# Last square of the second norm summed on TensorE and its spread read from PSUM; query and key transposes moved to the two banks of the scores

## The chip, the core and the metric

The kernel runs on one core of a Trainium2 chip. It is one program. The metric is its time on the device in microseconds (us). Before the change the median of three runs is 3415.19 us (3414.32 to 3415.7).

## The reference

Two transformer-like blocks run one after the other on one sequence of 512 tokens, width 1024, in float32. The first block has a conv branch, a gated linear recurrence (hgrn) and a stick-breaking attention, merged by gates, and after it a norm and a squared-ReLU feed-forward. The second block has two layers, each with a SwiGLU feed-forward, a mixer of softmax attention with a forget gate beside an RG-LRU recurrence, and a second SwiGLU. Cut to what the change touches:

```python
# first block, between its mixer and its feed-forward
x = x + g1 * (merged @ w_out[l])
h2 = rms_norm(x, norm2_g[l]) * (1.0 + sc2) + sh2      # mean of squares over the 1024 channels
x = x + g2 * (square(relu(h2 @ mlp_w1[l])) @ mlp_w2[l])

# second block, the mixer of each of two layers
q = rms_norm_2(q.reshape(B, S, 8, 128), q_norm[l])    # per head
k = rms_norm_2(k.reshape(B, S, 8, 128), k_norm[l])
y_attn = forgetting_attention(q, k, v, log_f) @ w_o_attn[l]
xr = causal_depthwise_conv(xr, conv_w[l], conv_b[l])  # 4 taps
yr = rg_lru(xr, ...) * gelu(gr)                       # two gates, then a scan over the positions
```

## The kernel before

Activations are held transposed: a tile `x` has 128 channels on the partitions and the 512 tokens in the free dimension, and the width of 1024 is eight such tiles. Weights stream from HBM in chunks of 128x512. Each chunk lands in a `raw` tile, ScalarE casts it to `hi` (line 197) and VectorE takes the rest `lo = raw - hi` (line 198); the ring of `raw`, `hi` and `lo` holds four chunks each. A product is three TensorE matmuls into an accumulator `a` (lines 229 to 231). There are four accumulators `a`, one PSUM bank each; the other four banks are, in the second block, one `xm`, one `xh` and two `xs` (`self.banks(..., xm=1, xh=1, xs=2)` in `run`); in the first block they are two `xh` and two `xs`.

**Order.** A tile belongs to a tag with a number of buffers. Tiles of one tag take the buffers in turn, in the order in which the program asks for them, and a tile waits until the tile that had its buffer before is read for the last time. When the kernel is built, a scheduler fixes the order of instructions on every engine by its own timing; work under `self.hp()` is taken first when ready, the rest in program order. On the chip each engine follows its fixed order and waits at an instruction whose inputs are not there, with all that stands behind it.

**The second norm.** `add_square` squares each new `x` tile on ScalarE (line 300) and adds it to the running sum `p` on VectorE (line 308). `stats` sums `p` over the partitions on TensorE (`rows_of`, line 272), takes the power -1/2 on GpSimd (line 281), spreads the row of factors over the partitions by four transposes (`spread`, line 289) and copies them from PSUM to the tile `rb` (line 291). Then eight `t` (line 588) and `h` (lines 590 and 591) are made from it, and the feed-forward's products read `h`.

**The mixer of the second block.** In `mix`, the recurrence `rnn` asks for its tiles first: per channel tile j = 0 to 7 a convolution of four taps on VectorE into `xc` (lines 893 and 895), two gate matmuls into two `xs` tiles (lines 897 and 898), a tanh of each (lines 900 and 901), an exponential, a second tanh and a square on ScalarE (lines 902, 903, 300), and two combining operations on VectorE (lines 905 and 906). After each four tiles come the square roots (line 911), and on VectorE a multiplication (913) and a scan over the positions (914). `xc` has three buffers and is also the tile of the square, so that tile j+2 of the convolution reuses what tile j held.

Then, for each half `hf` of the heads, the tokens of query, key and value are computed (`tokens`, four accumulators, eight chunks). VectorE takes them out of PSUM (line 1027), for query and key into `qk` tiles, of which there are five. `heads_T` norms them (lines 300, 381, 383, 384, 388) and transposes them on TensorE, four 128x128 blocks per tile, into a PSUM tile (line 393) that ScalarE copies to `qkT` (line 395). `attn` then runs 16 steps per half: scores into `xs` (line 830), softmax (833 to 841), transposes of the weights into `xs` (851), a copy (853) and the values into `xh` (855). While it runs, TensorE fills in the products that stand next in the program: those of the gelu gate, then query, key and value of the second half.

Of the kernel before, what the change touches and what calls it, by code (L numbers as in the profile page):

```python
# [16 lines left out]
D, S, F1, F2 = 1024, 512, 4096, 2816  # L17
# [7 lines left out]
def _cols(name, l, kt, c0):  # L25
    return [(name, l, k, 2, c0, 256) for k in range(0, kt, 2)]
# [6 lines left out]
def _plan_first():  # L33
    p = []
    for k in range(8):
        p += [("w_in", 0, k, 1, 1280, 512), ("w_in", 0, k, 1, 1792, 256)]
    p += _cols("w_in", 0, 8, 1024)
    p += _rows("w_in", 0, 8, 2048)
    for c in (512, 0, 768, 256):
        p += _cols("w_in", 0, 8, c)  # L40
    for c in (3072, 3584, 4096):
        p += _rows("w_in", 0, 8, c)
    for c in (2560, 2816):
        p += _cols("w_in", 0, 8, c)
    for b, w in BRANCHES:
        for m in range(0, 8, 2):
            p += _cols("w_in", 0, 8, 4608 + b * 1024 + m * 128)
            p += _cols(w, 0, 4, m * 128)
    for m in range(0, 8, 2):
        p += _cols("w_out", 0, 8, m * 128)  # L50
    for hf in range(2):
        for f in range(0, 16, 4):
            p += _both(*[_cols("mlp_w1", 0, 8, (hf * 16 + f + e) * 128) for e in (0, 2)])
        for m in range(0, 8, 2):
            p += [("mlp_w2", 0, hf * 16 + k, 2, m * 128, 256) for k in range(0, 16, 2)]
    return p
# [62 lines left out]
class Build:  # L119
# [148 lines left out]
    def rows_of(self, p, scale, xt="xm"):  # L268
# [4 lines left out]
                                  start=True, stop=True)  # L273
        return ps[:, 0:4]

    def rsqrt(self, src, w, g="m"):

        nc = self.nc
        m, r = self.small(w, g), self.small(w, g)
        nc.vector.tensor_scalar(m, src, EPS, None, op0=OP.add)  # L280
        nc.gpsimd.tensor_tensor(r, m, self.mhalf[:, :w], op=OP.pow)
        return r

    def spread(self, rt, xt="xm", tr="rb"):

        nc = self.nc
        ps = self.aux(xt)
        for i in range(4):
            nc.tensor.transpose(ps[:, i * 128:i * 128 + 128], rt[:, i:i + 1].to_broadcast([128, 128]), self.ident)
        rb = self.t(tr)  # L290
        nc.scalar.copy(rb, ps)
        return rb
# [83 lines left out]
    def heads_T_(self, src, nh, dh, gain):  # L376
        nc = self.nc
        ms, m, r = [self.small(4 * nh) for _ in range(3)]
        for tt in range(4):
            sq = self.square(src[tt], "t")  # L380
            nc.vector.tensor_reduce(ms[:, tt * nh:tt * nh + nh], sq.rearrange("p (h d) -> p h d", d=dh),
                                    op=OP.add, axis=AX.X)
        nc.vector.tensor_scalar(m, ms, 1.0 / dh, EPS, op0=OP.mult, op1=OP.add)
        nc.gpsimd.tensor_tensor(r, m, self.mhalf[:, :4 * nh], op=OP.pow)
        for tt in range(4):
            y = src[tt].rearrange("p (h d) -> p h d", d=dh)
            rr = r[:, tt * nh:tt * nh + nh][:, :, None].to_broadcast([128, nh, dh])
            nc.vector.tensor_tensor(y, y, rr, op=OP.mult)
        out = []
        for j in range(4):  # L390
            ps = self.aux("xm" if "xm" in self.pxt else "xs")
            for tt in range(4):
                nc.tensor.transpose(ps[:, tt * 128:tt * 128 + 128], src[tt][:, j * 128:j * 128 + 128], self.ident)  # L393
            o = self.t("qkT")
            nc.scalar.activation(o, ps, AF.Copy, scale=gain)
            out.append(o)
        return out
# [163 lines left out]
    def first_block(self):  # L561
        nc = self.nc
        src = lambda i: self.ap["xT"][i * 128:i * 128 + 128, :]
        with ExitStack() as ctx:
            fp = ctx.enter_context(self.tc.tile_pool(name="fp", bufs=1))
            self.banks(ctx, xh=2, xs=2)
            self.stream("w_first", _plan_first())
            self.mod = self.lined(fp, (128, 48), name="mod")
            self.cs = self.lined(fp, (128, 1024), name="cs")
            with ExitStack() as c1:  # L570
                mg = self.first_mix(c1, fp, src)
                with self.hp():
                    mh = [self.split(y, "Y") for y in mg]
                    self.load_x(src)
                x = self.x
                for m in range(0, 8, 2):
                    for i, a in enumerate(self.pair("w_out", 0, 8, m * 128, mh)):
                        with self.hp():
                            nc.vector.scalar_tensor_tensor(x[m + i], a, self.mod[:, 16 + m + i:17 + m + i], x[m + i],
                                                           op0=OP.mult, op1=OP.add)  # L580
                            self.add_square(x[m + i], m + i == 0)
            self.pool(ctx, "mlp", act=32, t=4, mr=2)
            with self.hp():
                _, rb = self.stats()
                h2 = []
                for i in range(8):
                    y, sh = self.t("t"), self.mod[:, 24 + i:25 + i]
                    nc.vector.scalar_tensor_tensor(y, x[i], self.mod[:, 32 + i:33 + i], rb, op0=OP.mult, op1=OP.mult)
                    hi, lo = self.t("h", F32R), self.t("h", F32R)
                    nc.scalar.activation(hi, y, AF.Identity, bias=sh)  # L590
                    nc.vector.scalar_tensor_tensor(lo, y, sh, hi.bitcast(F32), op0=OP.add, op1=OP.subtract)
                    h2.append((hi, lo))
            self.later("mod", [lambda j=j: self.mod_rest(j) for j in range(24, 32)], 0.2)
            self.later("mod", [self.decay_rates], 0.2)
            for hf in range(2):
                act = []
                for f in range(0, 16, 4):
                    for a in self.pairs(*[_cols("mlp_w1", 0, 8, (hf * 16 + f + e) * 128) for e in (0, 2)], h2):
                        y = self.t("t")
                        with self.hp():  # L600
                            nc.scalar.activation(y, a, AF.Relu)
                            nc.vector.tensor_tensor(y, y, y, op=OP.mult)
                            act.append(self.split(y, "act"))
                for m in range(0, 8, 2):
                    accs = [self.acc(), self.acc()]
                    for k in range(0, 16, 2):
                        self.cols(accs, ("mlp_w2", 0, hf * 16 + k, 2, m * 128, 256), hf * 16, hf * 16 + 15, act)
                    for i, a in enumerate(accs):
                        with self.hp():
                            nc.vector.scalar_tensor_tensor(x[m + i], a, self.mod[:, 40 + m + i:41 + m + i], x[m + i],  # L610
                                                           op0=OP.mult, op1=OP.add)
                            if hf:
                                self.ready(m + i, ("ffn1_norm_2", 0))
# [558 lines left out]
```

## Time and profile before

| | before |
|---|---|
| median of three runs | 3415.19 us |
| profiled execution | 3415.62 us |
| its span | 3413.8 us |
| busy: TensorE, VectorE, ScalarE, GpSimd | 3393.3, 1880.3, 1308.8, 164.6 us |
| granted TensorE clock, mean | 0.997 |

The profile is of one execution; its own time is 1.8 us above its span, and 0.43 us above the median. Its page gives the busy time of each engine, the chain of work that ended last and the costliest groups of instructions. A busy share of a matmul engine counts overlapping, pipelined matmuls, so how long a matmul holds the engine is read from the distance between the starts of two rows in the timeline, not from the duration in one row. A value in square brackets at the end of a timeline row is the time that the engine idled before it, with what ended the wait.

### The profile page before, as it was taken

Reading aid. Unit: us, or ns where it says so; the run is one execution under the profiler, and the core shown is the slowest. Engines: PE = TensorE matmul, PEld = TensorE weight load, DVE = VectorE, ACT = ScalarE, POOL = GpSimd, SP = SyncE. Lnnn points to the kernel's source line nnn. Section 1 sums busy time; section 2 is a strip of 40 time slices with the busy share of each in tenths; the row PEclk is TensorE's granted clock in tenths of the full one; section 3 lists DMA queues with packets and bytes.
Section 4 is the critical chain, followed back from the end, with each engine's and each line's share of the span. In section 5 each row is a group of like instructions: output and inputs, shape, how many; then the busy total and the mean of one; then the engine's idle time right before and its main releaser. Section 6 shows DMA issues by size and latency. Waiting matters only on the chain.

```text
span 3413.8 us, 42019 instructions
## 1 busy us (share of the span) xinstructions
PE 3393.3 (99%) x15370; PEld 2769.7 (81%) x15370; DVE 1880.3 (55%) x3168; ACT 1308.8 (38%) x2284; POOL 164.6 (5%) x273
## 2 busy tenths in 40 slices
PE   9999999999999999999999999999999999999999
PEld 6887777888888888788888888888887788888887
DVE  7698654534444444876455444444447865454442
ACT  3335443423333333654333333333336544343331
POOL 0011100000000001121000000000010110000000
PEclk9999999999999999999999999999999999999999
DMA  6223533433333333232333333333333222433332
GB/s 217 72 75 105 155 112 111 130 96 97 98 95 94 97 118 106 89 91 90 112 96 96 97 98 96 96 97 99 102 124 94 87 90 81 122 95 99 96 104 91
DMA packets 179599, 351.30 MB, mean 103 GB/s; under 512 B 20672, under 2 KB 21952, under 8 KB 178368
## 3 DMA queue, kind: packets, MB, share of 16 engines
q1 hardware_dynamic: 172944, 328.53, 31.5%
q0 software_dynamic: 6160, 19.37, 1.9%
q8 instruction: 121, 1.98, 0.2%
q10 hardware_dynamic: 288, 0.72, 0.1%
q14 instruction: 86, 0.70, 0.1%
HBM read 342.21 MB, written 6.32 MB: 102 GB/s over the span
## 4 chain that ended last, share of the span: by engine, by line
PE 97%; DVE 2%; ACT 1%; issue 0%; DMA 0%; POOL 0%; SPq 0%; DVEq 0%; ACTq 0%
PE a L231 30%; PE a L229 30%; PE a L230 30%; PE xh L855 1%; PE xs L830 1%; PE xh L430 1%; PE xh L512 1%; PE xs L490 1%; PE xs L851 1%; PE xm L393 0%; DVE xc L895 0%; PE xh L506 0%; PE xh L469 0%; PE xs L897 0%; PE xs L898 0%
## 5 line engine op out<-in xcount | busy, mean ns | idle before, releaser
L198 DVE TENSOR_TENSOR lo<-raw,hi 128x512 fp32r<-128x512 f32 x1144 | 785.8, 688 | 1255.9 <-ACT hi L197 1240.4
L197 ACT CAST hi<-raw 128x512 fp32r<-128x512 f32 x1144 | 707.1, 619 | 1569.4 <-PE a L230 1271.2
L230 PE MATMUL a<-h,hi 128*128 128x512 f32 x2528 | 990.3, 392 | 0.0
L229 PE MATMUL a<-h,hi 128*128 128x512 f32 x2528 | 984.6, 392 | 2.3 <-ACT h L590 2.3
L231 PE MATMUL a<-h,lo 128*128 128x512 f32 x2528 | 983.3, 393 | 0.0
L229 PEld LDWEIGHTS a<-h,hi 128*128 128x128 f32 x2528 | 475.5, 188 | 106.1 <-issue 6.1
L231 PEld LDWEIGHTS a<-h,lo 128*128 128x128 f32 x2528 | 475.2, 188 | 105.4 <-issue 7.2
L230 PEld LDWEIGHTS a<-h,hi 128*128 128x128 f32 x2528 | 475.2, 188 | 101.5 <-issue 3.6
L229 PE MATMUL a<-act,hi 128*128 128x512 f32 x960 | 373.4, 389 | 0.0
L230 PE MATMUL a<-act,hi 128*128 128x512 f32 x960 | 373.4, 389 | 0.0
L231 PE MATMUL a<-act,lo 128*128 128x512 f32 x960 | 372.8, 389 | 0.0
L230 PE MATMUL a<-Y,hi 128*128 128x512 f32 x544 | 214.5, 394 | 0.0
L229 PE MATMUL a<-Y,hi 128*128 128x512 f32 x544 | 213.7, 393 | 0.0
L231 PE MATMUL a<-Y,lo 128*128 128x512 f32 x544 | 212.8, 391 | 0.0
L230 PEld LDWEIGHTS a<-act,hi 128*128 128x128 f32 x960 | 180.2, 188 | 37.4
L229 PEld LDWEIGHTS a<-act,hi 128*128 128x128 f32 x960 | 180.2, 188 | 37.4
L231 PEld LDWEIGHTS a<-act,lo 128*128 128x128 f32 x960 | 180.2, 188 | 37.4
L231 PE MATMUL a<-hi,h 128*128 128x512 f32 x512 | 204.6, 403 | 0.0
L230 PE MATMUL a<-lo,h 128*128 128x512 f32 x512 | 203.7, 398 | 0.0
L229 PE MATMUL a<-hi,h 128*128 128x512 f32 x512 | 199.2, 407 | 1.7 <-DVE qk L1027 1.7
L231 PEld LDWEIGHTS a<-Y,lo 128*128 128x128 f32 x544 | 102.2, 188 | 23.6 <-issue 2.1
L230 PEld LDWEIGHTS a<-Y,hi 128*128 128x128 f32 x544 | 102.1, 188 | 22.9 <-issue 2.0
(290 smaller groups left out, 3056.7 us busy)
## 6 DMA issues: line engine op xcount, KB each, us to landing
raw<-in_w_l SPq DMA_DIRECT2D x852, 256.0 KB, 2.6
raw<-in_w_first SPq DMA_DIRECT2D x284, 256.0 KB, 2.6
mr<-in_mod_b_ SPq DMA_DIRECT2D x32, 512.0 KB, 3.8
mq<-in_mod_a SPq DMA_DIRECT2D x8, 1024.0 KB, 7.5
xs<-x POOLq DMA_DIRECT2D x16, 256.0 KB, 2.3
cb<-cd POOLq DMA_DIRECT2D x16, 256.0 KB, 3.5
x<-xs POOLq DMA_DIRECT2D x16, 256.0 KB, 3.8
bq<-in_brow POOLq DMA_DIRECT2D x12, 256.0 KB, 3.8
```

Source lines behind the costliest of these rows:

```text
L197: nc.scalar.copy(hi, raw)
L198: nc.vector.tensor_tensor(lo, raw, hi.bitcast(F32), op=OP.subtract)
L229: mm(acc, w[0], x[0], start=start, stop=False)
L230: mm(acc, w[0], x[1], start=False, stop=False)
L231: mm(acc, w[1], x[0], start=False, stop=stop)
L430: mm(ps[:, i * 64:i * 64 + 64], k[:, s], q[:, s].rearrange("p (n c h) -> p n c h", c=2, h=h)[:, :, 1], start=True, stop=True)
L490: mm(z[:, o:o + n], q[pr, blk(i)], k[pr, :n], start=True, stop=True)
L512: mm(pt[pr, c], v[j][:, hd * 64:hd * 64 + 64], f[:, o + j * 128:o + j * 128 + 128], start=j == 0, stop=j == i, skip_group_check=True)
L830: nc.tensor.matmul(ps[:, :n], qT[:, ts], kT[:, :n], start=True, stop=True)
L851: nc.tensor.transpose(pt[:, js], st[:, js], self.ident)
L855: nc.tensor.matmul(o[:, i * 128:n], v[j][:, vc:vc + 128], pT[:, j * 128:j * 128 + 128], start=(i == 0 and j == 0), stop=(i == 3 and j == 3 ...
```

## The change

In the second norm the eighth square is no longer added on VectorE. TensorE sums over the partitions both the sum of the first seven squares and the eighth square, eight matmuls of one column into the same accumulator columns, and the spread factors stay in PSUM, where the eight operations of line 588 read them. In `heads_T_` the PSUM tile of the query and key transposes is always of the tag `xs`; before, it was `xm` where that tag exists, which is in the second block, and `xs` in the first.

```diff
+    def rows_of_sum(self, parts, scale, xt):
+
+        ps = self.aux(xt)
+        for n, p in enumerate(parts):
+            for i in range(4):
+                self.nc.tensor.matmul(ps[:, i:i + 1], p[:, i * 128:i * 128 + 128], self.ones[scale][:, 0:1],
+                                      start=n == i == 0, stop=n == len(parts) - 1, skip_group_check=True)
+        return ps[:, 0:4]
...
-    def spread(self, rt, xt="xm", tr="rb"):
+    def spread(self, rt, xt="xm", tr="rb", out=True):
...
+        if not out:
+            return ps
         rb = self.t(tr)
         nc.scalar.copy(rb, ps)
         return rb
...
-            ps = self.aux("xm" if "xm" in self.pxt else "xs")
+            ps = self.aux("xs")
             for tt in range(4):
                 nc.tensor.transpose(ps[:, tt * 128:tt * 128 + 128], src[tt][:, j * 128:j * 128 + 128], self.ident)
...
-                            self.add_square(x[m + i], m + i == 0)
+                            if m + i < 7:
+                                self.add_square(x[m + i], m + i == 0)
...
-                _, rb = self.stats()
+                ps = self.rows_of_sum([self.p, self.square(x[7])], 1.0 / D, "xh")
+                rb = self.spread(self.rsqrt(ps, 4), "xh", out=False)
```

Lines behind the edits have other numbers in the changed kernel: 393 becomes 404, 897 and 898 become 910 and 911, 905 and 906 become 918 and 919, 913 and 914 become 926 and 927, 1027 becomes 1040, 851 and 855 become 864 and 868. The edit to the transposes also moves instructions. The first place is TensorE in the mixer of the first layer, first half of the heads. Here `xs` pairs with `xc,bd` are the gate matmuls of the recurrence's tiles 5, 6 and 7, rows from `qk` are transposes of the query, and `a` rows are products of the value tokens. Before:

```order
L897 MATMUL xs_11107<-xc_11102,bd_10639 128x512
L898 MATMUL xs_11108<-xc_11102,bd_10647 128x512
L229 MATMUL a_11646<-hi_11652,h_9922 128x512
...
L393 MATMUL xm_11423<-cst,qk_11380 128x128
...
L393 MATMUL xm_11430<-cst,qk_11386 128x128
L229 MATMUL a_11647<-hi_11652,h_9922 128x512
...
L897 MATMUL xs_11127<-xc_11122,bd_10639 128x512
L898 MATMUL xs_11128<-xc_11122,bd_10647 128x512
...
L897 MATMUL xs_11147<-xc_11142,bd_10639 128x512
L898 MATMUL xs_11148<-xc_11142,bd_10647 128x512
```

And now:

```order
L910 MATMUL xs_11108<-xc_11103,bd_10640 128x512
L911 MATMUL xs_11109<-xc_11103,bd_10648 128x512
L229 MATMUL a_11647<-hi_11653,h_9923 128x512
...
L910 MATMUL xs_11128<-xc_11123,bd_10640 128x512
L911 MATMUL xs_11129<-xc_11123,bd_10648 128x512
L910 MATMUL xs_11148<-xc_11143,bd_10640 128x512
L911 MATMUL xs_11149<-xc_11143,bd_10648 128x512
L404 MATMUL xs_11410<-cst,qk_11381 128x128
...
L404 MATMUL xs_11417<-cst,qk_11381 128x128
...
L404 MATMUL xs_11431<-cst,qk_11387 128x128
L229 MATMUL a_11648<-hi_11653,h_9923 128x512
```

Before, there are products between the pairs of tiles 5, 6 and 7 (39 `a` rows between 5 and 6, and 51 between 6 and 7, with transposes among them). Now 12 `a` rows stand between tiles 5 and 6, none between 6 and 7, and all 16 transposes of the query follow in one piece before the next `a` row.

The second place is VectorE at the same time. `xc` rows are taps of the convolution (tile 6 in the first fence, tile 7 in the second), `abc` rows with `xc` are the combining operations, `hm` rows the scans, and the rows into `qk` take key tokens 1 to 3 out of PSUM. Before:

```order
L893 TENSOR_SCALAR xc_11122<-xr_10982,cv 128x512
...
L895 SCALAR_TENSOR_TENSOR xc_11122<-xr_10982,cv,xc_11122 128x512
L1027 SCALAR_TENSOR_TENSOR qk_11589<-a_11440,m_10617,bq_11437 128x512
L1027 SCALAR_TENSOR_TENSOR qk_11591<-a_11441,m_10617,bq_11437 128x512
L1027 SCALAR_TENSOR_TENSOR qk_11593<-a_11442,m_10617,bq_11437 128x512
```

And now:

```order
L908 SCALAR_TENSOR_TENSOR xc_11143<-xr_10988,cv,xc_11143 128x512
L918 SCALAR_TENSOR_TENSOR abc_11133<-xc_11139,abc_11133 128x512
L908 SCALAR_TENSOR_TENSOR xc_11143<-xr_10988,cv,xc_11143 128x512
L919 SCALAR_TENSOR_TENSOR abc_11132<-abc_11132,xc_11123 128x512
L908 SCALAR_TENSOR_TENSOR xc_11143<-xr_10988,cv,xc_11143 128x512
...
L927 SCALAR_TENSOR_TENSOR hm_11094<-hm_11094,abc_11092 128x512
...
L926 TENSOR_TENSOR abc_11152<-abc_11152,abc_11153 128x512
L927 SCALAR_TENSOR_TENSOR hm_11134<-hm_11134,abc_11132 128x512
L1040 SCALAR_TENSOR_TENSOR qk_11590<-a_11441,m_10618,bq_11438 128x512
```

Key tokens 1 to 3 left PSUM during the convolution of tile 6 before; now they stand behind the whole recurrence: the convolutions of tiles 6 and 7, four multiplications and three scans.

The third place is TensorE at the end of the attention of the first half, with the query transposes of the second half. Rows 864 transpose the weights of a step, rows 868 are its values, and `a_12798` and `a_12799` are the first two accumulators of the second half's value tokens. Before, where rows 855 are the values, 851 the weights and `a` rows products of the key tokens:

```order
L393 MATMUL xm_12560<-cst,qk_12531 128x128
L229 MATMUL a_12592<-hi_12650,h_10155 128x512
...
L393 MATMUL xm_12567<-cst,qk_12531 128x128
...
L855 MATMUL xh_12018<-pT_12063,v_11794 128x128
...
L393 MATMUL xm_12574<-cst,qk_12531 128x128
...
L393 MATMUL xm_12581<-cst,qk_12537 128x128
L855 MATMUL xh_12018<-pT_12089,v_11800 128x128
```

And now:

```order
L868 MATMUL xh_12112<-pT_12157,v_11795 128x128
...
L864 MATMUL xs_12162<-cst,s_12141 128x128
L404 MATMUL xs_12561<-cst,qk_12532 128x128
...
L864 MATMUL xs_12162<-cst,s_12141 128x128 x3
L404 MATMUL xs_12568<-cst,qk_12532 128x128
...
L868 MATMUL xh_12112<-pT_12167,v_11795 128x128
...
L404 MATMUL xs_12582<-cst,qk_12538 128x128
L229 MATMUL a_12799<-hi_12804,h_9923 128x512
```

Before, the same transposes were spread over the third of the half's four heads, with `a` rows between them; now they stand at the end of the fourth, with no `a` row among them. The second layer has the same order at the same places.

## Rows read from the trace of the kernel before

**Rows 1.** The page, its chain of work that ended last, by engine.

```profile
PE 97%; DVE 2%; ACT 1%; issue 0%; DMA 0%; POOL 0%; SPq 0%; DVEq 0%; ACTq 0%
```

**Rows 2.** Waits of TensorE in total: engine, line, releaser, us, times, longest.

```profile
PE a L229 <- DVE qk L1027: 1.7, 2, 0.9
...
PE xm L393 <- ACT qkT L395: 0.8, 2, 0.4
```

**Rows 3.** Timeline at the second norm: start, us, engine, line, tiles, [idle before].

```profile
586.97 0.68 DVE L308 TENSOR_TENSOR p<-p,sq 128x512 f32<-128x512 f32 x1
...
589.00 1.02 PE L272 MATMUL xh<-oned,p 128*128 128x1 f32 x8 [2.74 <-DVE p L308]
...
592.55 0.59 ACT L291 COPY rb<-xh 128x512 f32<-128x512 f32 x1 [4.77 <-PE xh L289]
593.17 2.74 DVE L588 SCALAR_TENSOR_TENSOR t<-x,mod,rb 128x512 f32<-128x512 f32 x4 [2.95 <-ACT rb L291]
...
597.22 0.63 PE L231 MATMUL a<-h,lo 128*128 128x512 f32 x1
...
597.65 0.63 PE L229 MATMUL a<-h,hi 128*128 128x512 f32 x1
```

**Rows 4.** Stretches behind it: engines' busy us, granted clock, DMA share, GB/s.

```profile
596.00:600.00 4.00, 4.00 (x11) 2.84 (x10) 4.00 (x7) 1.47 (x4) 0.00 (x0) 0.50 0.02 4
600.00:604.00 4.00, 4.00 (x18) 3.23 (x18) 4.00 (x7) 3.06 (x5) 0.00 (x0) 0.96 0.00 0
```

**Rows 5.** Timeline of TensorE, first layer, transposes and gates among the products.

```profile
1410.02 0.60 PE L393 MATMUL xm<-cst,qk 128*128 128x128 f32 x4
1410.46 1.02 PE L897 MATMUL xs<-xc,bd 128*128 128x512 f32 x2
1411.32 1.02 PE L898 MATMUL xs<-xc,bd 128*128 128x512 f32 x2
1411.78 0.80 PE L229 MATMUL a<-hi,h 128*128 128x512 f32 x1
1412.41 0.39 PE L230 MATMUL a<-lo,h 128*128 128x512 f32 x1
1412.64 0.39 PE L231 MATMUL a<-hi,h 128*128 128x512 f32 x1
...
1423.67 1.02 PE L897 MATMUL xs<-xc,bd 128*128 128x512 f32 x2
```

**Rows 6.** Timeline of VectorE in the same stretch.

```profile
1392.94 1.29 DVE L913 TENSOR_TENSOR abc<-abc,abc 128x512 f32<-128x512 f32 x2
...
1397.72 2.34 DVE L914 TENSOR_TENSOR_SCAN hm<-hm,abc 128x512 f32<-128x512 f32 x2
...
1408.88 0.75 DVE L895 SCALAR_TENSOR_TENSOR xc<-xr,cv,xc 128x512 f32<-128x512 f32 x1
1409.54 0.75 DVE L1027 SCALAR_TENSOR_TENSOR qk<-a,m,bq 128x512 f32<-128x512 f32 x1
...
1414.08 0.69 DVE L906 SCALAR_TENSOR_TENSOR abc<-abc,xc 128x512 f32<-128x512 f32 x1 [1.35 <-ACT abc L901]
```

**Rows 7.** Timeline of ScalarE in the same stretch.

```profile
1389.71 1.28 ACT L911 ACT_TABLE_LOAD   x1
1391.00 2.20 ACT L911 ACTIVATE abc<-abc 128x512 f32<-128x512 f32 x4
...
1411.94 0.68 ACT L900 ACTIVATE abc<-xs,hb 128x512 f32<-128x512 f32 x1
...
1415.18 0.67 ACT L395 ACTIVATE qkT<-xm,qg 128x512 f32<-128x512 f32 x1
...
1424.73 0.69 ACT L900 ACTIVATE abc<-xs,hb 128x512 f32<-128x512 f32 x1 [0.24 <-PE xs L897]
```

**Rows 8.** Timeline of one attention step of the first half, softmax of 512 columns.

```profile
1512.15 0.71 ACT L839 ACTIVATE s<-s,m 128x512 f32<-128x512 f32 x1
...
1513.18 0.49 DVE L841 TENSOR_SCALAR s<-s,m 128x512 f32<-128x512 f32 x1
```

## The prediction

> **What bounds the kernel now.** I read the chain of waits first: 97% of it is TensorE [rows 1]. Then the waits of TensorE: in the mixer of the second block it waits only four times in the whole run, twice 0.86 us for VectorE taking a key token out of PSUM and twice 0.38 us for ScalarE emptying the one transpose bank [rows 2]. So a change is worth what it takes from or adds to TensorE's waits; time on another engine counts only where TensorE reaches an instruction whose inputs that engine has not made. Last, the timelines of the three places that the order shows to be changed. Prices are distances between starts: a product 0.23 us, a gate matmul 0.86 (two rows), four transposes 0.44, and the first product behind a gate pair 0.63 instead of 0.23 [rows 5].
>
> **The second norm.** The chain here is serial, and TensorE waits in it. One VectorE addition goes, but TensorE gets eight sums where it had four: the four of `p` can start when the sixth addition ends (586.97 + 0.68, against 589.00: with the hop 1.2 us sooner), and the added four cost about 1 us (the old four are eight matmul rows in 1.02) [rows 3]. I take 0.3 us gained; between 1 us gained (the sums of `p` fully hidden) and nothing. The copy to `rb` goes: line 588 starts 0.62 us after that copy did [rows 3], and can now start about there: 0.6 us gained. An operation of 588 from PSUM is bounded by 1027, which reads PSUM and takes 0.75 us, against 2.74 us for four of 588, 0.69 each: nothing to 0.06 us on the first one. Sum: 0.9 us gained.
>
> **Transposes, first half of the heads (twice, once in each layer).** On `xm` the transposes depended only on the tokens. On `xs` they take the banks behind the last gate pair, so the query's transposes wait for all eight tiles of the recurrence. The key tokens need the query's `qk` buffers (five for eight tiles), so three of the four key accumulators cannot be emptied, and TensorE has one free accumulator for the value tokens: 12 products (four chunks), then nothing to fill in. I walk through the new order on the clock of this trace.
>
> - Tile 5. Its last tap starts at 1408.88 and takes 0.75 [rows 6]; its gates start at 1409.7, and TensorE, which has 32 key products before it, waits 0.2 us. Two gates (1.72), then 12 products (0.63 + 11 x 0.23): TensorE is through at 1414.6.
> - Tile 6. ScalarE has a square and a cast ahead, so the tanh of tile 5 starts about 1412.1. From tanh to the end of the square is 3.24 us plus a tenth (from 1411.94 to 1415.18, [rows 7]). VectorE then does one combining operation (0.6) and the last two taps (0.66 and 0.75): 1417.6, gates at 1417.7. **Wait 3.1.** Before, the same work was late too: 1.35 us of VectorE's waiting [rows 6] stood behind products.
> - Tile 7. The tanh starts 1.06 us after the gate does (1423.67 to 1424.73, [rows 5, 7]). Tanh, exponential, tanh, square without the gate's own second tanh (0.55) take 2.75. Then in VectorE's new order a combining operation, a tap, another combining operation, a tap: 0.6 + 0.66 + 0.6 + 0.75. With the hops 6.6 us from gate to gate: gates at 1424.3. TensorE works 1.72 of that. **Wait 4.9.**
> - Transposes. The first tile's bank is free in time, done 1426.5. The second needs the bank of tile 7's second gate, read last on ScalarE: 1424.3 + 1.06 + 3.34 = 1428.7. **Wait 2.4.** The third needs the first's copy, which stands behind a table load (1.28) and three of four roots (2.20 for four, [rows 7]): 1428.7 + 1.3 + 1.65 + 0.7, **wait 3.0**; the fourth waits 0.65 for the second's copy and ends at 1433.9.
> - Key token 1 leaves PSUM behind four multiplications (1.29 for two) and three scans (2.34 for two, [rows 6]) that start with the first root at 1430.5: 1430.5 + 2.4 + 3.4 + 0.75 = 1437.1. **Wait 3.3.**
>
> Sum 17.6 us. Off come the waits of before, 0.86 + 0.38 = 1.24 [rows 2], and 1.2 us because TensorE changes less often between transposes or gates and products: two gate pairs no longer have a product behind them (2 x 0.40) and about five groups of transposes (0.09 each, my estimate).
>
> [...]
>
> [...]
>
> So 17.6 - 2.4 + 2.7 = 17.9 us.
>
> **Transposes, second half of the heads (also twice).** The query's transposes must now follow the attention of the first half. TensorE runs out of products in the last three steps: 13, 10, 2 and 0 stand there. From the exponential of 512 columns to the finished weights are 1.03 + 0.49 us [rows 8], and ScalarE does the copy for the third step's values only behind that exponential: wait 1.35. The second transpose group waits 1.1 for two copies of 0.6, the first value product behind the transposes 0.7 for one key token to leave PSUM (0.75). Sum 3.2, less 0.4 for fewer changes: 2.8 us. Bounds: 0.5 (only the last wait) and 7 (all three with a fallen clock).
>
> The transposes' own gain, a second bank, is the 0.38 us that is already taken off above. SP issues what it did, in the same order, and GpSimd's rows move only with the attention; neither is near the end of a chain here.
>
> **Sum.** 2 x (17.9 + 2.8) - 0.9 = 40.5 us. On the profiled execution's 3415.62 that is 3456.1; this execution is 0.43 above the median, so 3456 us, 1.2% slower.
>
> **Rivals.**
> - *Slack, not slower.* The fixed order puts tile 7's gates where they are because VectorE, with no key tokens to empty, does the recurrence earlier. If its tiles were ready when TensorE arrives, all waits would go and those of before too: 3415.2 - 0.9 - 2 x (1.24 + 1.6) = 3408.6. For it: VectorE does have less before tile 6. Against it: tile 7 needs the square of tile 5 (three `xc` buffers) and, in VectorE's order, that of tile 6, and a gate-to-gate round of 6.6 us with 1.7 us of TensorE's work is a chain that nothing fills. It decides if tile 6's taps end before 1414.6. Chance 0.09.
> - *Shorter waits.* ScalarE and VectorE reach their instructions sooner than I think, so that tile 6 and the copies behind the roots cost nothing: tile 7's 4.9, 2 at the transposes and the 3.3 of the key token remain, with 1 for the clock: 2 x (10.2 - 2.4 + 1 + 2.8) - 0.9 = 22, so 3438. Chance 0.14. Against it: ScalarE and VectorE take their rows in the order shown.
> - *The low clock lasts.* [...] Chance 0.17.
>
> **How the numbers follow.** The forecast has 0.60. Range 3432 to 3473: from the shorter waits to the lasting clock. About 0.2% (6.8 us) is what a measurement of this kernel can tell from no change. The slack case lies at its edge (-6.6 us): I give faster 0.03, the same 0.07, and slower 0.90.
>
> **What would show it.** Right: in both mixers TensorE waits for VectorE's `xc` about 3 and 5 us, for ScalarE's copies and tanh 2 to 3 us, and 3 us at a value product for the `qk` row 1040; a granted clock under 1 between those; TensorE's busy time in the two stretches some 15 us less. At the second norm the copy of line 291 gone and the first product 0.9 us sooner. Wrong: no wait over 1 us at the gates, or the time lost elsewhere than in the two mixers.

## The result and the profile after

| | before | after |
|---|---|---|
| median | 3415.30 us (4 runs) | 3457.18 us (4 runs, 3456.39 to 3457.98) |
| ratio to before | | 1.0123, 95% interval 1.0111 to 1.0136 |
| profiled execution, its span | 3415.62, 3413.8 us | 3457.40, 3455.6 us |
| granted TensorE clock, mean | 0.997 | 0.991 |

The change costs 41.9 us; 3456 was forecast. The waits of TensorE in the changed kernel, as engine, line, releaser, us in total, times, longest:

```profile
PE xs L910 <- DVE xc L908: 14.7, 4, 4.3
PE a L229 <- DVE qk L1040: 6.5, 4, 2.7
PE xs L404 <- ACT qkT L406: 6.2, 4, 2.9
...
PE xs L404 <- ACT abc L914: 2.4, 2, 1.4
```

The two rows that stood there for the mixers [rows 2] came to 2.5 us. Now the gates wait for the convolution four times (twice in each layer), the transposes for ScalarE, and a value product for a key token: 30 us in all, these four rows together. That is less than the 43 us or so that the mixers lost (the 41.9 and what the norm gained); most of the rest is no wait but TensorE's own work, which took longer where the granted clock was low (in the first layer at 0.50 from 1416 to 1420 us and 0.51 from 1436 to 1440: gates start 1.28 and 1.84 us apart instead of 0.86, products 0.43 instead of 0.23).

The timeline of TensorE in the first layer, first half of the heads, with the products left out except one. Start, us, engine, line, tiles, and in brackets the idle time before a row:

```profile
1407.56 1.10 PE L910 MATMUL xs<-xc,bd 128*128 128x512 f32 x2
...
1415.45 1.49 PE L910 MATMUL xs<-xc,bd 128*128 128x512 f32 x2 [3.18 <-DVE xc L908]
1416.73 1.92 PE L911 MATMUL xs<-xc,bd 128*128 128x512 f32 x2
1422.67 2.05 PE L910 MATMUL xs<-xc,bd 128*128 128x512 f32 x2 [4.02 <-DVE xc L908]
1424.51 1.89 PE L911 MATMUL xs<-xc,bd 128*128 128x512 f32 x2
1426.22 0.62 PE L404 MATMUL xs<-cst,qk 128*128 128x128 f32 x4
1428.28 0.66 PE L404 MATMUL xs<-cst,qk 128*128 128x128 f32 x4 [1.44 <-ACT abc L914]
1431.84 2.21 PE L404 MATMUL xs<-cst,qk 128*128 128x128 f32 x8 [2.90 <-ACT qkT L406]
1436.76 0.80 PE L229 MATMUL a<-hi,h 128*128 128x512 f32 x1 [2.71 <-DVE qk L1040]
```

The same sequence as in [rows 5], but each step waits. From gate to gate, tile 6 to tile 7, pass 7.22 us. In the second layer pass 7.90 us: there the order is not quite the same, the two combining operations stand the other way round on VectorE and the tanh of the second gate comes sooner on ScalarE. What TensorE waits for is read on ScalarE,

```profile
1416.98 0.69 ACT L913 ACTIVATE abc<-xs,hb 128x512 f32<-128x512 f32 x1 [3.89 <-PE xs L910]
...
1424.76 0.69 ACT L913 ACTIVATE abc<-xs,hb 128x512 f32<-128x512 f32 x1 [4.31 <-PE xs L910]
...
1428.25 1.28 ACT L924 ACT_TABLE_LOAD   x1
1429.54 1.67 ACT L924 ACTIVATE abc<-abc 128x512 f32<-128x512 f32 x3
1431.12 0.67 ACT L406 ACTIVATE qkT<-xs,qg 128x512 f32<-128x512 f32 x1
```

and on VectorE:

```profile
1419.91 0.69 DVE L918 SCALAR_TENSOR_TENSOR abc<-xc,abc 128x512 f32<-128x512 f32 x1 [3.36 <-ACT xc L311]
...
1421.78 0.74 DVE L908 SCALAR_TENSOR_TENSOR xc<-xr,cv,xc 128x512 f32<-128x512 f32 x1
...
1434.85 1.22 DVE L927 TENSOR_TENSOR_SCAN hm<-hm,abc 128x512 f32<-128x512 f32 x1
1435.98 2.04 DVE L1040 SCALAR_TENSOR_TENSOR qk<-a,m,bq 128x512 f32<-128x512 f32 x3
```

All three engines idle in turn: ScalarE 3.9 and 4.3 us for a gate, VectorE 3.36 us for a square, TensorE for the tap that ends at 1422.5. The key tokens leave PSUM right behind the third scan, 1435.98, and the first value product starts 0.78 us later. The third transpose group follows the first copy, which stands behind the table load and three roots.

The granted clock in this place (busy us of PE, PEld, DVE, ACT, POOL, then clock, DMA share, GB/s):

```profile
1412.00:1416.00 4.00, 0.82 (x4) 0.34 (x3) 3.93 (x7) 1.09 (x2) 0.00 (x0) 1.00 0.11 41
1416.00:1420.00 4.00, 2.65 (x4) 0.56 (x2) 0.64 (x2) 2.95 (x5) 0.00 (x0) 0.50 0.00 0
...
1436.00:1440.00 4.00, 3.24 (x8) 2.56 (x9) 4.00 (x7) 1.89 (x3) 0.59 (x1) 0.51 0.06 22
1440.00:1444.00 4.00, 4.00 (x19) 3.30 (x18) 1.09 (x3) 0.01 (x1) 2.72 (x1) 1.00 0.16 44
```

After the wait of 3.18 us the clock is down to 0.50 already during the gates of tile 6: from the first gate to the second pass 1.28 us instead of 0.86, and the tanh starts 1.53 us after the gate; for tile 7 it is 2.09 us (1.06 in [rows 5, 7]). The first products behind the waits still run at 0.51, and six of them start 0.43 us apart.

At the second norm the timeline of the changed kernel reads:

```profile
587.69 1.02 PE L281 MATMUL xh<-oned,p 128*128 128x1 f32 x8 [1.53 <-DVE p L319]
...
588.57 1.03 PE L281 MATMUL xh<-oned,sq 128*128 128x1 f32 x8
...
592.13 2.72 DVE L601 SCALAR_TENSOR_TENSOR t<-x,mod,xh 128x512 f32<-128x512 f32 x4 [2.33 <-PE xh L298]
```

The sums start 1.3 us sooner than in [rows 3] and take twice as long; the operations on `x` start at 592.13 instead of 593.17. Everything ahead of it was 0.1 us earlier in this execution, so 0.9 us are the change's. Four of these operations from PSUM take 2.72 us, from SBUF they took 2.74. In the second half of the heads the waits are short:

```profile
1548.01 0.94 PE L868 MATMUL xh<-pT,v 128*128 128x128 f32 x6 [0.15 <-ACT pT L866]
...
1550.27 1.14 PE L404 MATMUL xs<-cst,qk 128*128 128x128 f32 x8 [0.45 <-ACT qkT L406]
...
1553.26 0.50 PE L229 MATMUL a<-hi,h 128*128 128x512 f32 x1 [0.52 <-DVE qk L1040]
```

### The profile page after: what moved, and what is told of

Read it like the earlier page. It is cut to its first block, busy times and chain, and to the rows that moved or that the text cites. A ratio compares the mean times of both kernels' runs of the same rounds, so it can differ in the third digit from the quotient of the medians.

```text
span 3455.6 us, 42041 instructions
## 1 busy us (share of the span) xinstructions
PE 3409.1 (99%) x15378; PEld 2777.2 (80%) x15378; DVE 1882.1 (54%) x3167; ACT 1310.3 (38%) x2283; POOL 156.1 (5%) x273
## 4 chain that ended last, share of the span: by engine, by line
PE 95%; DVE 3%; ACT 1%; issue 1%; DMA 0%; POOL 0%; SPq 0%; DVEq 0%; ACTq 0%
PE a L231 29%; PE a L229 29%; PE a L230 29%; PE xh L868 1%; PE xs L843 1%; PE xh L441 1%; PE xh L523 1%; PE xs L501 1%; PE xs L864 0%; DVE xc L908 0%; PE xs L404 0%; PE xs L910 0%; DVE hm L927 0%; DVE lo L198 0%; PE xh L517 0%
## 5 line engine op out<-in xcount | busy, mean ns | idle before, releaser
L229 PEld LDWEIGHTS a<-hi,h 128*128 128x128 f32 x512 | 97.1, 190 | 30.2 <-DVE qk L1040 8.2
```

The lines of the kernel that those rows point to most:

```text
L229: mm(acc, w[0], x[0], start=start, stop=False)
```

## The experiments

Theory: the query's transposes, put on the banks of the scores, must follow the recurrence; three key accumulators then cannot be emptied, TensorE has nothing to fill in, and it waits for a chain through ScalarE and VectorE, which its own low clock lengthens. Rivals: the loss is at the end of the attention; it is TensorE's own work or order; the norm's edit takes part in it.

**The edit of the norm alone.**

```diff
-            ps = self.aux("xs")
+            ps = self.aux("xm" if "xm" in self.pxt else "xs")
             for tt in range(4):
```

> The changed kernel with the transposes back on the one bank xm; only the edit of the second norm is left. Theory (the loss is the transposes'): the time of the kernel before less what the norm gives, 2.2 us by the shift that the changed kernel's trace shows at the first mixer (0.9 us in the prediction): 3413 us. Rival (the norm's edit loses too, or moves the order elsewhere): 3415 or more.

Measured: 3414.28 us (11 runs), beside 3415.26 of before (21 runs); ratio 0.9997, interval 0.9989 to 1.0006. The norm's edit is not where the loss is. Its gain is 1.0 us by the medians, which the interval (3.8 us gained to 2.0 lost) does not tell from none. The 2.2 us of the expectation took the profiled executions at their word: there the clock was back sooner behind the norm (from 596 to 600 us 0.90 in the changed kernel and 0.86 in this one, against 0.50 in [rows 4]), and the timed runs do not give that much. The last kernel below has the same norm and reads 0.51 there, so the sooner clock cannot be put down to the edit.

**The transposes alone.** The kernel before, with the same line edited the other way.

```diff
-            ps = self.aux("xm" if "xm" in self.pxt else "xs")
+            ps = self.aux("xs")
             for tt in range(4):
```

> The kernel before with only the transposes moved to the two banks of the scores. Theory: the whole loss and none of the norm's gain, 3457.2 + 2.2 = 3459 us. Rival (the two edits work on each other through the order): away from that by more than 2 us.

Measured: 3458.10 us, ratio 1.0127 (1.0113 to 1.0140): 42.8 us more than before. With the 1.0 us of the norm this is the changed kernel's 41.9 us. The two edits add up. In this kernel the gates of tile 6 in the first layer run at 1.00 behind a wait as long as the changed kernel's (3.17 us, there 3.18), and the clock falls only in the next wait (0.81 from 1420 to 1424 us):

```profile
1417.57 1.10 PE L897 MATMUL xs<-xc,bd 128*128 128x512 f32 x2 [3.17 <-DVE xc L895]
...
1424.40 2.04 PE L897 MATMUL xs<-xc,bd 128*128 128x512 f32 x2 [4.87 <-DVE xc L895]
```

```profile
1416.00:1420.00 4.00, 1.96 (x4) 0.68 (x4) 1.85 (x3) 1.26 (x2) 0.00 (x0) 1.00 0.00 0
1420.00:1424.00 4.00, 0.00 (x0) 0.00 (x0) 3.12 (x5) 2.04 (x4) 0.00 (x0) 0.81 0.00 0
```

From tile 5's gates to the first value product pass 28.80 us here and 29.20 in the changed kernel, so little hangs on which of the two it is.

**Only the first half of the heads through the scores' banks.**

```diff
-            ps = self.aux("xs")
+            ps = self.aux("xm" if "xm" in self.pxt and self.hf != 0 else "xs")
             for tt in range(4):
...
             for hf in range(2):
+                self.hf = hf
                 for n in range(3):
```

> The changed kernel, where only the first half of the heads in each layer transposes through the scores' banks and the second half uses xm again. Theory: the recurrence in front of the first half's transposes is nearly all of it, about 19.5 us in each of two layers by the trace: 3413 + 39 = 3452 us. Rival (the end of the attention is the larger part): under 3435.

Measured: 3454.08 us, ratio 1.0115 (1.0101 to 1.0129). That is 39.8 us over the norm's edit alone, 19.9 us in each layer. The loss is in front of the first half's transposes; the rival that puts it at the end of the attention is out.

**Only the second half.** The same edit with `self.hf != 1`.

> The reverse: only the second half of the heads uses the scores' banks. Theory: 2.5 us a layer, 3413 + 5 = 3418 us (waits of TensorE of about 1 us a layer in the trace would give 3415; the prediction's 2.8 a layer 3419). Rival: over 3430.

Measured: 3420.78 us, ratio 1.0017 (1.0008 to 1.0026): 6.5 us over the norm's edit alone, 3.25 us a layer, where 2.5 was expected. Added to the first half's 39.8 it is 46.3, and both together cost 42.9: behind a changed first half the second costs 1.55 a layer. The waits of this kernel show the difference:

```profile
1529.41 0.94 PE L868 MATMUL xh<-pT,v 128*128 128x128 f32 x6 [0.62 <-ACT pT L866]
1531.51 0.33 PE L864 MATMUL xs<-cst,s 128*128 128x128 f32 x1 [1.16 <-DVE s L854]
1533.05 1.13 PE L404 MATMUL xs<-cst,qk 128*128 128x128 f32 x8 [0.45 <-ACT qkT L406]
1536.03 0.50 PE L229 MATMUL a<-hi,h 128*128 128x512 f32 x1 [0.52 <-DVE qk L1041]
```

The last two are those of the changed kernel, to the hundredth; of the first two one was 0.15 there and one was none. Why the last softmax is later here was not tried.

**Work in the waits.** Matmuls of a gate's size behind the gates of tiles 5, 6 and 7, into the bank that the transposes left.

```diff
+    def fill(self, n, w, x):
+        ps = self.aux("xm")
+        for _ in range(n):
+            self.nc.tensor.matmul(ps, w, x, start=True, stop=True)
...
                 nc.tensor.matmul(gx, bd[1][j // 4][:, j % 4], xc, start=True, stop=True)
+                if j > 4:
+                    self.fill({5: 3, 6: 4, 7: 2}[j], bd[0][j // 4][:, j % 4], xc)
```

> The changed kernel with nine more gate-sized matmuls per layer on the free bank xm, whose results nobody reads: three behind the gates of tile 5, four behind those of tile 6, two behind those of tile 7. They are 9 x 0.86 = 7.7 us of TensorE's work a layer, in the places of the waits of 3.2, 4.0 and 1.4 us. Theory (TensorE is waiting for the chain through ScalarE and VectorE, and the low clock lengthens that chain): the added work costs nothing, and with the clock kept up the gates of tiles 6 and 7 take 0.5 and 1.0 us less on the chain and the products behind are not at the low clock: 3 to 6 us less than the changed kernel, 3451 to 3454 us. Rival (TensorE's own work or its order is what is longer): 2 x 7.7 more, 3472 us. Rival (waits as in the theory, but the clock costs nothing): 3457 us.

Measured: 3450.53 us, ratio to before 1.0103 (1.0089 to 1.0117), 6.65 us less than the changed kernel with 15.5 us more work. TensorE in this kernel:

```profile
1415.36 1.03 PE L915 MATMUL xs<-xc,bd 128*128 128x512 f32 x2
1416.22 1.02 PE L916 MATMUL xs<-xc,bd 128*128 128x512 f32 x2
1417.08 3.60 PE L898 MATMUL xm<-xc,bd 128*128 128x512 f32 x8
1422.11 1.10 PE L915 MATMUL xs<-xc,bd 128*128 128x512 f32 x2 [1.44 <-DVE xc L913]
...
1430.19 1.46 PE L404 MATMUL xs<-cst,qk 128*128 128x128 f32 x8 [3.19 <-ACT qkT L406]
1433.40 0.80 PE L229 MATMUL a<-hi,h 128*128 128x512 f32 x1 [1.75 <-DVE qk L1047]
```

and its clock:

```profile
1416.00:1420.00 4.00, 4.00 (x10) 1.71 (x9) 1.44 (x3) 3.30 (x5) 0.00 (x0) 1.00 0.00 0
1420.00:1424.00 4.00, 2.56 (x7) 0.96 (x6) 1.93 (x3) 0.72 (x2) 0.00 (x0) 1.00 0.00 0
...
1432.00:1436.00 4.00, 2.60 (x6) 2.13 (x7) 4.00 (x6) 1.26 (x3) 0.00 (x0) 0.50 0.00 0
```

The gates of tiles 6 and 7 start when they did in the changed kernel or sooner, with work where the waits were: 6.75 us from gate to gate instead of 7.22, and the first value product at 1433.40 instead of 1436.76. The clock stays at 1.00 through the gates, from 1412 to 1428 us, and falls only at the waits behind them, of 3.19 and 1.75 us (0.88 from 1428 to 1432 us, 0.50 from 1432 to 1436). So TensorE was waiting: 15.5 us of added work cost nothing, and the rival of TensorE's own work (3472 us) is out. The time lies 0.5 us under the range of the theory, and the clock is not all that gave it. What it gave is read on ScalarE:

```profile
1416.42 0.69 ACT L920 ACTIVATE abc<-xs,hb 128x512 f32<-128x512 f32 x1 [3.46 <-PE xs L915]
...
1423.25 0.69 ACT L920 ACTIVATE abc<-xs,hb 128x512 f32<-128x512 f32 x1 [3.49 <-PE xs L915]
```

The tanh starts 1.06 and 1.14 us behind the gate, where it was 1.53 and 2.09: 1.4 us less on the chain. But this edit moved instructions too. On VectorE key token 1 now leaves PSUM behind two scans instead of three:

```profile
1431.48 1.22 DVE L934 TENSOR_TENSOR_SCAN hm<-hm,abc 128x512 f32<-128x512 f32 x1
1432.62 0.72 DVE L1047 SCALAR_TENSOR_TENSOR qk<-a,m,bq 128x512 f32<-128x512 f32 x1
...
1433.86 1.22 DVE L934 TENSOR_TENSOR_SCAN hm<-hm,abc 128x512 f32<-128x512 f32 x1
```

From the first multiplication behind the roots to this row pass 4.07 us, in the changed kernel 5.78, in both layers. So of the 3.36 us by which the first value product comes sooner in the first layer, 1.7 are this order and some 1.4 the clock. A kernel with work in the waits and the old order was not run; that the clock costs time on the chain is shown by the starts of the tanh, not by the 6.65 us.

**Buffers instead of banks, with a control.** The control is the changed kernel with smaller pools:

```diff
-            self.pool(ctx, f"mb{l}", hm=8, t=3, bq=1, qk=5, v=6, qkT=8, cb=2, s=3, pT=2)
+            self.pool(ctx, f"mb{l}", hm=8, t=2, bq=1, qk=5, v=4, qkT=8, cb=2, s=3, pT=2)
```

> Control for the next run: the changed kernel with four buffers instead of six for value tokens and two instead of three for the tile t, so that the next one has room. Both theories: within 5 us of the changed kernel, 3452 to 3462 us; whatever it is, the next run is compared with it.

Measured: 3463.62 us, ratio 1.0141 (1.0127 to 1.0154). The smaller pools cost 6.4 us by themselves, a little more than expected. The next kernel has `qk=8` in that line and nothing else changed:

> As the control, with eight qk buffers instead of five: the key tokens can leave PSUM before the query is transposed, so TensorE has the 96 value products and those of the gelu gate to fill in while the recurrence runs. The transposes still wait for the recurrence, on the same two banks. Theory (the loss is the missing filler, through the qk buffers): most of the 20 us a layer goes, 30 to 42 us less than the control, 3416 to 3427 us. Rival (transposes behind the recurrence cost the time by themselves, through the later attention): less than 15 us off.

Measured: 3427.42 us, ratio 1.0035 (1.0022 to 1.0049): 36.2 us less than the control, within the 30 to 42 expected (the time itself is 0.4 us over its range, since the control was slower than thought). Its transposes are on the two banks of the scores, behind the recurrence, as in the control; the last gates start later (1438.40), and TensorE no longer waits for the convolution anywhere:

```profile
1426.66 1.02 PE L910 MATMUL xs<-xc,bd 128*128 128x512 f32 x2
...
1438.40 1.02 PE L910 MATMUL xs<-xc,bd 128*128 128x512 f32 x2
...
1444.47 0.60 PE L404 MATMUL xs<-cst,qk 128*128 128x128 f32 x4
```

So it is not the late transposes that cost the time but that nothing could fill in: the key tokens held three accumulators for want of a `qk` buffer. The 13.1 us by which this kernel stays above the norm's edit alone are about what two other things cost by themselves: the second half of the heads 6.5, whose waits (2.3, 1.2 and 0.9 us in total) stand here as in the kernel with that half alone, and the smaller pools 6.4, with a wait of 1.8 us a layer for VectorE's tile `ct` that only this kernel and the control have. That the two simply add was not tried.

**Two banks that nobody asks for.** The norm's edit stays; the transposes of the first half alternate between `xm` and `xh`, which is idle until the attention; those of the second half use `xm`.

```diff
-            ps = self.aux("xs")
+            ps = self.aux(("xm", "xh")[j % 2] if "xm" in self.pxt and self.hf == 0 else "xm" if "xm" in self.pxt else "xs")
             for tt in range(4):
```

> The norm's edit kept, and two banks for the transposes taken where nothing else asks for them: in the first half of the heads the transposes alternate between xm and xh, in the second half they use xm. Theory: no wait for the recurrence or the attention, and the waits of before at the one bank (0.86 and 0.38 us in each layer) go: 2.5 us under the 3414.3 of the norm's edit alone, 3411.8 us. Rival (the second bank gives nothing, since products fill in behind a single bank): 3414.3 us.

Measured: 3410.66 us (11 runs), ratio 0.9985 (0.9976 to 0.9994). It beats both kernels: 4.8 us under before, 3.6 under the norm's edit alone. The longest waits left on TensorE are of the norms and the start:

```profile
PE xs L230 <- DVE h L659: 3.9, 4, 1.5
PE xh L298 <- POOL m L290: 3.6, 2, 2.3
```

Both rows of the mixers [rows 2], 2.5 us, are gone from the list. The gain over the norm's edit is 1.1 us more than these; what it comes from was not tried.

## Why the prediction was right, point by point

- **The second norm.** 0.3 us for the sums and 0.6 for the copy were forecast; the trace has 0.3 and 0.6 (0.9 together), the timed runs 1.0. An operation that reads the factors from PSUM costs what it did (four of them 2.72 us, from SBUF 2.74).
- **First half of the heads, 17.9 us a layer.** Measured 19.9, by the kernel with that half alone. The steps were the right ones, in the right order, with the right releasers. Their sizes: 3.1 for tile 6 (3.18 in the trace), 4.9 for tile 7 (4.02), 2.4 and 3.0 at the transposes (1.44 and 2.90), 3.3 for the key token (2.71). The waits came out shorter, but the chain did not: TensorE was slower at its own work meanwhile (gates 1.28 and 1.84 us apart instead of 0.86). From tile 5's gates to the first value product pass 29.2 us (1407.56 to 1436.76); the walk had 27.4 (1409.7 to 1437.1).
- **The clock, 2.7 us a layer.** The sum has it as my estimate; no run shows this term, and what the runs showed in its place is a clock of 0.50 during tile 6's gates in the changed kernel (1416 to 1420 us), and with the transposes alone 1.00 there and a fall in front of tile 7's gates (0.81 from 1420 to 1424 us). What that cost is, by the rows of the changed kernel, as much as the term in the first layer and more in the second. In the first they give 0.47 and 1.03 us on the chain (the tanh 1.53 and 2.09 us behind the gate, not 1.06) and 0.2 on each of six products that start 0.43 us apart behind the last wait: 2.7. In the second they give 0.86 and 1.02 us and eleven such products: 4.1. The mean of 3.4 is an estimate from these rows; it is 0.7 of the 2 us that the half was above the forecast, and where the rest comes from is not shown. The filled kernel gave 3.3 us a layer back, but about half of that is its order. Behind the wait of 3.18 us the clock read 0.50, and 1.00 where that wait was filled with work. Not every such wait ends in a low clock: with the transposes alone it read 1.00 behind one of 3.17 us.
- **Second half, 2.8 us a layer.** 1.55 in the changed kernel, 3.25 alone. The wait of 1.35 us for the copy behind the exponential was 0.15, the 1.1 at the second transpose group 0.45, the 0.7 for the key token 0.52. I had put both copies, the first group's and that of the weights, in front of the second group at their full length.
- **The sum.** 3456 forecast, 3457.18 measured. That it is this close is luck, since two errors cancel: the second half was 2.5 us too dear over both layers, the first half 4.0 us too cheap. The mechanism is not luck: each half was measured by itself.
- **The rivals.** The slack case needed tile 6's taps done by 1414.6; they ended at 1415.3 in a kernel that ran 2 us ahead, so some 3 us late. The case of shorter waits fell with tile 6's wait of 3.18 us, which it put at nothing, and with the table load and the roots, which stood where the order had them. The lasting clock was my estimate too, and came true in part: the clock was low from tile 6 to the value products (0.50 to 0.72 in each 4 us from 1416 to 1440 us), but not at the end of the attention, where it stayed at 1.00 (1536 to 1560 us).

## What to carry to other kernels

Tiles of one tag take their buffers in program order, so moving a tile to a tag with more buffers also puts it behind every earlier user of that tag; look at who these are and what they wait for before counting the banks. A late consumer costs nothing as long as the busiest engine has other work whose buffers are free: here three `qk` buffers were worth 36 us, and a second bank that nobody asked for 3.6. When the busiest engine does wait, as TensorE did here for 3.18 and 4.02 us in front of gates, read its granted clock there (0.50 here), and add to the chain what the clock loses (here 0.47 and 1.03 us). And an edit that only adds work can still move the order of other engines: compare the orders before putting the whole gain down to one cause.

## What the runs showed of the hardware

Work whose result nobody reads cost nothing here: nine matmuls of 0.86 us in each layer's waits, and the kernel was 6.65 us faster, partly by TensorE's clock and partly by an order that moved with them. A low clock of TensorE lengthened a chain that is mostly on other engines: at 0.50, gates that start 1.28 and 1.84 us apart instead of 0.86 put off ScalarE's tanh by 0.47 and 1.03 us, though three quarters of the 7.22 us from gate to gate are on other engines. A wait of some 3 us did not settle the clock behind it: after 3.18 us it read 0.50 during the gates in one kernel (1416 to 1420 us), after 3.17 it read 1.00 in the same 4 us in another. Four operations of VectorE that read the factors from PSUM took 2.72 us, from SBUF 2.74.
